# Giving SyncE's transfers the program-order edge that the other engines' instructions have, in a one-core hybrid decoder step

## The chip, the cores and the metric

The kernel runs on one core of a Trainium2 chip. The core has a matrix engine (PE, with its weight loads shown apart as PEld), VectorE (DVE), ScalarE (ACT), GpSimd (POOL) and SyncE (SP). In this kernel SP computes nothing: it issues all transfers between the chip's memory and the core's on-chip memory, one after the other, into one hardware queue (SPq in the profile), and 16 DMA engines carry them out. The metric is the device time of one execution in microseconds, the median of three runs; lower is better.

## What is computed

One inference step of a decoder with two layers of width 1024, for a prompt of 1024 rows and a sample group of 8 x 4 rows (1056 rows in all). Both layers are `x <- x + gate * Branch(RMSNorm(x) * (1 + scale) + shift)`; the first branch is attention in a sliding window, the second a gated DeltaNet (gated linear attention in chunks of 64 with a state for each head). Cut to what matters here:

```python
for layer in range(DEPTH):                       # 0: window attention, 1: gated DeltaNet
    hp, gp = modulate(xp, c_prompt, ...); hs, gs = modulate(xs, c_sample, ...)
    if layer % 2 == 0:
        op, kp, vp = swa_branch(hp, w_in, sinks, w_out)                    # prompt
        osm, ks, vs = swa_branch(hs, w_in, sinks, w_out, cache_k, cache_v) # sample, with its cache
    else:
        op, cp, sp = gdn_branch(hp, zeros, zeros, w_in, conv_w, ..., w_out)
        osm, cs, ss = gdn_branch(hs, state_conv, state_s, w_in, conv_w, ..., w_out)
    xp, xs = xp + gp * op, xs + gs * osm
y_prompt, y_sample = rms_norm(xp, final_norm_g), rms_norm(xs, final_norm_g)

# inside a DeltaNet branch, for each of 16 heads and each chunk of 64 rows:
lower = strict_lower((kb @ k.T) * decay)
sol   = triangular_solve(lower + I, [v * beta, kb * exp(g)])
u     = sol_v - sol_k @ S
o     = q_dec @ S + (q @ k.T * decay) @ u
S     = S * exp(g_total) + k_dec.T @ u          # S: 128 x 128 for each head (and each sample row group)
```

The outputs are the two `y`, the new caches, the new convolution states, and the new states `S` of the prompt (16 heads) and of the eight sample sequences (8 x 16 heads, 64 KB each).

## The kernel before

The work runs in stages along the span. From 0 to about 115 us the inputs are loaded and normalised and the first projections run. Up to about 530 us it is layer 0: projections, attention over blocks of 128 rows, the output projection, with its result kept in memory (`x1d`). From about 530 to 1440 us it is the head loop of layer 1: for each of eight pairs of heads the projections of q, k, v and z, the short convolution, the decay tables, the inversion of the 64 x 64 triangles, and the chain over the chunks. From about 1440 us to the end the output projection of layer 1 runs over the nine row blocks twice (heads 0 to 7, stored in `x2d`, then heads 8 to 15, which gives `y`), and beside it the sample states are read, updated and stored.

Every float32 product is made from split operands (a high part cast by ACT, a low part from POOL or DVE, three matmuls), so that a weight tile goes through load `wr`, cast `wh`, difference `wl`.

**What sets the order.** From the attention on, the kernel issues everything through a planner, the class `Core` (line 96). Each instruction passes through `Core.issued` (line 111), which keeps for each engine the time at which it is free and for each tile the times at which it is written and last used, in a model of the engines. Generators (`weave`) yield the time or the condition at which they want to go on (`ready`, `soon`, `idle`), and the planner places their next instruction when the model says that its moment has come. In that model a transfer occupies SP for 0.45 us and is there 2.4 us after its start, SP works in program order, and a transfer that overwrites something that a transfer last used is not made to wait for it (line 124). For PE, ACT, DVE and POOL the order so found is then made binding: lines 145 to 149 add an edge (without a semaphore) from each instruction to the one before it on its engine. For transfers (lines 126 to 128) no such edge is added. Their place in SP's queue is set afterwards by the tile scheduler, which puts an instruction in when its own model finds its operands and its buffer free; two transfers with no tie between them can change places.

On SP a transfer whose operand or buffer isn't ready holds everything behind it in the queue.

**The names that the prediction touches.**

- `wr` (`load_raw`, line 441, and `load_out`, line 2111): raw weight tiles, a ring of four buffers. `wh`, `wl` (`split_w`, line 449) free them.
- `DP` (`decay_blocks`, line 1786): decay tables, 128 x 2 x 2 x 128 for each of four chunk groups, loaded from `gcr` by eight transfers and then worked on by DVE.
- `Ld` (`solve`), `X`, `Xdd`, `Xc` (`invert`, line 1884): the triangles of a head pair are stored to `Ld`, read back as `X` with one triangle on each partition, inverted by DVE, stored to `Xdd`, read back as `Xc`.
- `zl` (`gating`, line 1993): the gate of a chunk group, loaded from `zd`, multiplied in, and stored to `gTd`; one buffer. `of` (`prepare`, line 2198) reads `gTd` back for the output projection, two buffers.
- `xt` (`rows_of`, line 2231; `finish`, line 2245): the rows of a block, loaded from `x1d` or `x2d`, two buffers; stored to `x2d` or to the output `y`.
- `S` in `new_states` (line 2624): sample states, a ring of three buffers (4 heads each, later 8). After a unit is stored, the next `fetch` reads into the buffer that this store empties:

```python
for _ in range(2):
    fetch()
while units:
    fetch()                                     # loads st <- state_gdn_s
    b, h0, n, st = units.pop(0)
    ...                                         # matmul, then DVE S <- S, gtb, ps_mi
    nc.sync.dma_start(S1[b][:, h0:h0 + n], st)  # out_new_s_s <- S
```

and the rows of a block are asked for when the block before the last has been stored:

```python
yield lambda: stored[0] >= b - 1
xt = xts_[b] = x3.tile([P, D], F32, tag="xt", name="xt", bufs=2)
nc.sync.dma_start(xt[0:cs.stop - cs.start], (x2d if part else x1d)[cs])
```

Of the kernel before, what the change touches and what calls it, by code (L numbers as in the profile page):

```python
# [95 lines left out]
class Core:  # L96
# [14 lines left out]
    def issued(self, eng, op, ins, args, kwargs):  # L111
        aps = [a for a in (*args, *kwargs.values()) if hasattr(a, "tensor")]
        outs = [a for a in (kwargs.get("out", aps[0]), kwargs.get("accum_out")) if a is not None]
        srcs = [a for a in aps if not any(a is o for o in outs)]
        n = 1
        for d in outs[0].shape[1:]:
            n *= d
        start = self.free[eng]
        for a in srcs:
            start = max(start, self.after(self.written, a, eng))  # L120
            if a.space == PSUM:
                start = max(start, self.after(self.used, a, eng))
        for a in outs:
            if self.used.get(self.key(a), (0.0, ""))[1] != "sync" or eng != "sync":
                start = max(start, self.after(self.used, a, eng))
        if "dma" in op:
            self.free[eng] = start + 0.45
            end = start + 2.4
        else:
            rate, fixed = {"tensor": (2400 if op == "matmul" and srcs[0].dtype == F32R  # L130
                                      else 1200 if op == "transpose" else 600, 0.004),
                           "scalar": (1200, 0.06 if op == "copy" and srcs[0].space == PSUM else 0.14
                                      if srcs and srcs[0].space == PSUM else 0.18),
                           "vector": (960, 0.13 if op == "scalar_tensor_tensor" else 0.08),
                           "gpsimd": (420, 0.02 if n >= 256 else 0.14)}[eng]
            if op == "matmul" and outs[0].shape[0] <= 64 and srcs[0].dtype == F32:
                rate = 2400 if n <= 64 and outs[0].shape[0] <= 32 else 600 * P / outs[0].shape[0] if self.group != outs[0].offset // outs[0].ap[0][0] else rate
            if eng == "tensor":
                self.group = outs[0].offset // outs[0].ap[0][0]
            if op == "tensor_scalar_mul" and srcs and srcs[0].space != PSUM and eng == "vector":  # L140
                rate = 1920
            if op == "memset":
                rate = 1e9
            end = self.free[eng] = start + fixed + n / rate
            if eng in self.last:
                self.tc.add_manual_dep(ins, self.last[eng],
                                       mybir.DependencyInfo(mybir.DependencyClass.NoSync, mybir.DependencyReason.DATA),
                                       reason="program order")
            self.last[eng] = ins.name
        for a in srcs:  # L150
            self.used[self.key(a)] = max(self.used.get(self.key(a), (0.0, "")), (end, eng))
        for a in outs:
            self.written[self.key(a)] = self.used[self.key(a)] = (end, eng)
# [2565 lines left out]
```

## Time and profile before

| | |
|---|---|
| time, median of 3 runs | 1733.99 us (1732.49 to 1739.18) |
| profiled execution, its own time | 1732.34 us |
| its span, from the first to the last instruction | 1730.6 us |
| mean granted clock of PE | 0.982 |
| moved by DMA | 191.82 MB |
| transfers read and written in memory | 144.68 MB read, 47.04 MB written |

How to read it: the profile's page gives each engine's busy time as a share of the span, a picture of the span in 40 slices (each digit the busy share in tenths), the chain of work that ended last, and groups of instructions. Views of the trace show the same for a stretch: the instructions in order of time with what ended the idle time before them, the waits of one engine summed by what it waited for, and the busy time of each engine by window. In all of them L89 is the line of the wrapper through which the planner issues, so instructions are told apart by tile names (out<-in). For SP's queue the second column is the time in which the queue was occupied with issuing, for a DMA in the chain of waits it is the time from issue to landing.

### The profile page before, as it was taken

To read this page: it belongs to the slowest core of one execution; us is meant where nothing else is said; L and a number is where in the kernel's file an instruction comes from. 1 tells how busy PE (TensorE), PEld (TensorE's weight loads), DVE (VectorE), ACT (ScalarE), POOL (GpSimd) and SP (SyncE) were. 2 spreads that over 40 slices of the span, in tenths; PEclk is the share of its full clock that TensorE was granted. 3 is DMA by queue.
4 is the path that set the end of the run, shared out by engine and by line. 5 is a ranking of instruction groups with operands and counts; after the bars stand their busy time and mean duration, and the time that the engine had idled before them with its cause. 6 is when DMAs were issued, how large, how long until landed. Compare 5 with 4: busy or idle time off the path is not lost. (4 is left out here: it accounts for less than half of the span.)

```text
span 1730.6 us, 32224 instructions
## 1 busy us (share of the span) xinstructions
PE 1621.2 (94%) x10666; PEld 1429.5 (83%) x10666; DVE 1174.6 (68%) x3538; ACT 862.6 (50%) x2514; POOL 675.5 (39%) x1576
## 2 busy tenths in 40 slices
PE   6999999999999999589999999999999998989897
PEld 5987888977788889469989999899999996657675
DVE  4426675555565787757878778778697776357676
ACT  5625555453335664166554655554655655332332
POOL 2601121122213356235544654546356565323332
PEclk9999999999999999799999999999999999999998
DMA  9542122234233323122412324224132237764885
GB/s 330 153 133 73 51 58 55 51 103 114 92 122 97 105 55 85 29 68 69 127 42 73 102 58 114 65 69 117 46 104 70 56 93 227 218 190 138 244 268 171
DMA packets 281577, 191.82 MB, mean 111 GB/s; under 512 B 98361, under 2 KB 253881, under 8 KB 281378
## 3 DMA queue, kind: packets, MB, share of 16 engines
q1 hardware_dynamic: 281410, 189.75, 38.2%
q8 instruction: 85, 1.39, 0.3%
q14 instruction: 82, 0.67, 0.1%
HBM read 144.68 MB, written 47.04 MB: 111 GB/s over the span
## 5 line engine op out<-in xcount | busy, mean ns | idle before, releaser
L89 POOL TENSOR_TENSOR wl<-wr,wh 128x128 fp32r<-128x128 f32 x488 | 236.7, 515 | 485.5 <-ACT wh L89 449.4
L89 PE MATMUL ps_pj<-h2hi,wh 128*128 128x384 f32 (+1 forms) x1128 | 379.9, 337 | 0.0
L89 PE MATMUL ps_pj<-h2lo,wh 128*128 128x384 f32 (+1 forms) x1128 | 378.1, 335 | 0.0
L89 PE MATMUL ps_pj<-h2hi,wl 128*128 128x384 f32 (+1 forms) x1128 | 376.8, 334 | 0.0
L89 PEld LDWEIGHTS ps_pj<-h2hi,wh 128*128 128x128 f32 x1128 | 213.2, 189 | 3.1 <-ACT wh L89 0.2
L89 PEld LDWEIGHTS ps_pj<-h2hi,wl 128*128 128x128 f32 x1128 | 213.2, 189 | 2.7 <-POOL wl L89 0.2
L89 PEld LDWEIGHTS ps_pj<-h2lo,wh 128*128 128x128 f32 x1128 | 213.0, 189 | 2.2
L89 POOL TENSOR_TENSOR xt<-xt,y 128x512 f32<-128x512 f32 (+1 forms) x48 | 63.6, 1328 | 194.3 <-DVE y L89 170.4
L89 PE MATMUL ps_pj<-hlo,wh 128*128 128x384 f32 (+1 forms) x360 | 119.1, 331 | 0.0
L89 PE MATMUL ps_pj<-hhi,wh 128*128 128x384 f32 (+1 forms) x360 | 118.4, 329 | 0.0
L89 PE MATMUL ps_pj<-hhi,wl 128*128 128x384 f32 (+1 forms) x360 | 118.1, 328 | 0.0
L89 DVE SCALAR_TENSOR_TENSOR vT<-XR,cT,vT 128x384 f32<-128x384 f32 (+1 forms) x144 | 83.9, 591 | 47.4 <-ACT vT L89 45.3
L89 DVE TENSOR_TENSOR tmp<-X 64x31 f32<-64x31 f32 (+15 forms) x248 | 89.0, 359 | 16.9 <-POOL X L89 13.4
L89 DVE TENSOR_TENSOR X<-X,tmp 64x31 f32<-64x31 f32 (+15 forms) x248 | 90.7, 366 | 8.5
L89 ACT CAST wh<-wr 128x512 fp32r<-128x512 f32 x122 | 75.1, 617 | 16.4 <-PE ps_pj L89 11.3
L89 POOL TENSOR_TENSOR Xd<-Xc,cst 32x128 f32<-32x128 f32 x128 | 62.7, 490 | 40.5 <-DVE UZ L89 24.4
L89 PEld LDWEIGHTS ps_pj<-hlo,wh 128*128 128x128 f32 x360 | 67.7, 188 | 10.5 <-issue 10.5
L89 ACT COPY XR<-ps_pj 128x384 f32<-128x384 f32 (+1 forms) x96 | 43.0, 448 | 59.5 <-PE ps_pj L89 59.4
L89 PEld LDWEIGHTS ps_pj<-hhi,wh 128*128 128x128 f32 x360 | 67.7, 188 | 4.0 <-issue 3.1
L89 ACT ACTIVATE prob<-prob,nm 128x256 f32<-128x256 f32 (+1 forms) x128 | 62.2, 489 | 15.5 <-DVE nm L89 15.3
L89 PEld LDWEIGHTS ps_pj<-hhi,wl 128*128 128x128 f32 x360 | 67.7, 188 | 2.2 <-issue 2.1
L89 ACT ACTIVATE qe<-ps_mi,Eg 128x128 f32<-128x128 f32 x112 | 34.9, 363 | 60.4 <-PE ps_mi L89 60.3
(574 smaller groups left out, 4203.9 us busy)
## 6 DMA issues: line engine op xcount, KB each, us to landing
wr<-in_gdn_w_in SPq DMA_DIRECT2D x96, 256.0 KB
S<-in_state_gdn_s SPq DMA_DIRECT2D x40, 256.0 KB
xt<-in_x_prompt SPq DMA_DIRECT2D x16, 512.0 KB
wm<-in_w_mod SPq DMA_DIRECT2D x16, 512.0 KB
wr<-in_swa_w_in SPq DMA_DIRECT2D x64, 128.0 KB
wmod<-in_w_mod SPq DMA_DIRECT2D x32, 256.0 KB
wm<-in_w_mod SPq DMA_DIRECT2D x32, 256.0 KB
DP<-gcr SPq DMA_DIRECT2D x64, 128.0 KB
```

What stands on the lines that cost most here:

```text
L89: inst = fn(*args, **kwargs)
```

## The change

In the branch for transfers, `Core.issued` now adds the same edge that the other engines' instructions have, to the instruction that the program issued last on the same engine, and notes the transfer as the last one. The planner's model, the times in it and the order of the program are as before.

```diff
         if "dma" in op:
             self.free[eng] = start + 0.45
             end = start + 2.4
+            if eng in self.last:
+                self.tc.add_manual_dep(ins, self.last[eng],
+                                       mybir.DependencyInfo(mybir.DependencyClass.NoSync, mybir.DependencyReason.DATA),
+                                       reason="program order")
+            self.last[eng] = ins.name
         else:
```

What moves: on SP the order changes almost everywhere from the attention on. On PE, DVE, ACT and POOL the order from there on is the same; ahead of it (up to about 115 us, outside the planner) a gate step and half of the sample rows' v transposes come some 28 instructions earlier. Three places of SP's queue follow, the operand names as in the list above.

SP, end of the program before (the last rows; `S_...` are single buffers of sample states, the last `of` loads are further up):

```order
L89 DMA xt<-x2d 128x1024
L89 DMA of<-gTd 128x4x128
L89 DMA S_20587<-in_state_gdn_s 128x8x128
L89 DMA out_new_s_s<-S_20394 128x8x128
L89 DMA S_20644<-in_state_gdn_s 128x8x128
L89 DMA out_new_s_s<-S_20496 128x8x128
L89 DMA out_y_p<-xt 128x1024
L89 DMA xt<-x2d 32x1024
L89 DMA out_new_s_s<-S_20587 128x8x128
L89 DMA out_y_p<-xt 128x1024
L89 DMA xt<-x2d 128x1024
```

SP, the same place in the change:

```order
L89 DMA out_new_s_s<-S_20332 128x8x128
L89 DMA S_20587<-in_state_gdn_s 128x8x128
L89 DMA out_new_s_s<-S_20394 128x8x128
L89 DMA S_20644<-in_state_gdn_s 128x8x128
L89 DMA out_new_s_s<-S_20496 128x8x128
L89 DMA out_y_p<-xt 128x1024
L89 DMA xt<-x2d 32x1024
L89 DMA of<-gTd 128x4x128 x2
L89 DMA out_new_s_s<-S_20587 128x8x128
L89 DMA out_y_p<-xt 128x1024
L89 DMA xt<-x2d 128x1024
```

The last two `of` loads, those of the last row block, now stand behind the load of the sample rows (`xt<-x2d 32x1024`), and so behind the `out_y_p` store that empties its buffer. In the rows above this place, too, each store is now followed at once by the load into the buffer that it empties.

SP, the first two head pairs of layer 1, before:

```order
L89 DMA Ld<-UZ 32x4x32 x8
L89 DMA zd<-th 128x384
L89 DMA Ld<-UZ 32x4x32 x8
L89 DMA zd<-th 128x384
L89 DMA zl<-zd 128x2x256
L89 DMA wr<-in_gdn_w_in 128x4x128
L89 DMA X<-Ld 64x1024
L89 DMA zd<-th 128x256
L89 DMA smd<-th 128x32
L89 DMA wr<-in_gdn_w_in 128x4x128 x2
```

SP, the same place in the change:

```order
L89 DMA Ld<-UZ 32x4x32 x8
L89 DMA zd<-th 128x384
L89 DMA Ld<-UZ 32x4x32 x8
L89 DMA X<-Ld 64x1024
L89 DMA zd<-th 128x384
L89 DMA zd<-th 128x256
L89 DMA smd<-th 128x32
L89 DMA DP<-gcr 128x256 x8
L89 DMA wr<-in_gdn_w_in 128x4x128 x2
```

`X<-Ld` comes directly behind the stores it reads, and the eight decay loads of the next head pair, of which most stood further up in pieces of two and three, stand together behind it.

SP, the end of layer 0's attention (`kc`, `vc` the sample caches; `wor` and `wr` weights of the output projection; `selt` a constant), before:

```order
L89 DMA wor<-in_swa_w_out 64x512 x10
L89 DMA kc<-in_cache_swa_k 128x2x256 x2
L89 DMA wr<-in_swa_w_out 64x512 x3
L89 DMA vc<-in_cache_swa_v 128x2x256
L89 DMA wr<-in_swa_w_out 64x512 x2
L89 DMA vc<-in_cache_swa_v 128x2x256
L89 DMA selt<-in_cst 128x256
```

SP, the same place in the change:

```order
L89 DMA wor<-in_swa_w_out 64x512 x10
L89 DMA kc<-in_cache_swa_k 128x2x256
L89 DMA vc<-in_cache_swa_v 128x2x256
L89 DMA kc<-in_cache_swa_k 128x2x256
L89 DMA vc<-in_cache_swa_v 128x2x256
L89 DMA selt<-in_cst 128x256
L89 DMA wr<-in_swa_w_out 64x512 x8
```

Eight halves of weight tiles that were loaded among the caches (three of them further up) now come behind `selt`.

## The prediction

> **What bounds the kernel now.** I read the page first: the busy shares, the slices of the DMA engines, and the chain that ended last.
>
> ```profile
> PE 1621.2 (94%) x10666; PEld 1429.5 (83%) x10666; DVE 1174.6 (68%) x3538; ACT 862.6 (50%) x2514; POOL 675.5 (39%) x1576
> DMA  9542122234233323122412324224132237764885
> PE 27%; DMA 5%; DVE 3%; ACT 2%; POOL 2%; issue 2%; SPq 1%; POOLq 0%; ACTq 0%; DVEq 0%
> ```
>
> PE is the bound: 94% busy, 109 us idle in all (1730.6 less 1621.2). The DMA engines are lightly used through most of the span (tenths 1 to 4) and heavily in the last eight slices, from about 1385 us on (7, 7, 6, 4, 8, 8, 5 behind a 3). An order of transfers can only save or cost where PE or its suppliers wait, so the second view is busy time by window.
>
> ```profile
> 0.00:100.00 100.00, 85.77 (x598) 75.22 (x599) 41.74 (x113) 51.90 (x99) 40.03 (x62) 0.98 0.74 238
> 650.00:750.00 100.00, 76.97 (x596) 67.52 (x595) 74.75 (x209) 31.44 (x101) 41.32 (x113) 0.88 0.24 57
> 750.00:1350.00 600.00, 581.17 (x4079) 551.02 (x4080) 466.50 (x1334) 348.06 (x1093) 308.23 (x869) 1.00 0.30 81
> 1450.00:1550.00 100.00, 91.03 (x485) 63.31 (x485) 44.82 (x131) 36.95 (x100) 33.41 (x67) 0.97 0.76 222
> 1600.00:1650.00 50.00, 44.74 (x198) 35.04 (x196) 34.19 (x97) 17.53 (x38) 17.12 (x14) 0.97 0.85 255
> 1650.00:1700.00 50.00, 48.49 (x224) 39.34 (x223) 35.24 (x126) 15.57 (x40) 15.16 (x12) 1.00 0.84 251
> 1700.00:1731.00 31.00, 17.92 (x79) 12.70 (x77) 21.66 (x71) 7.33 (x17) 5.42 (x4) 0.83 0.47 145
> ```
>
> Columns: window, length, busy of PE, PEld, DVE, ACT, POOL, granted clock, DMA share, GB/s. PE loses 14 us at the start, 23 us near 700, 19 us over the 600 us of the head loop behind it, 9 us at 1450 to 1550, and 20 us after 1600, where the DMA engines are 0.84 busy. The waits of PE over the whole span name what it waited for:
>
> ```profile
> PE ps_lg L89 <- DVE UZ L89: 19.0, 6, 16.9
> PE ps_lg L89 <- DMA S<-in_state_gdn_s: 5.3, 3, 2.3
> PE ps_mi L89 <- DMA kc<-in_cache_swa_k: 3.2, 2, 2.7
> ```
>
> Directly it waits little for transfers (8.5 us); its one long wait, 16.9 us, is for DVE's inversion. So the change acts through other engines, and above all through the time in which SP itself stands. The waits of SP's queue over the whole span, and then, in a second view, from 1600 us on:
>
> ```profile
> SPq L89 <- ACT wh L89: 191.0, 54, 16.2
> SPq L89 <- POOL wl L89: 148.6, 77, 5.9
> ```
>
> ```profile
> SPq L89 <- DMA out_new_s_s<-S: 31.9, 12, 7.0
> SPq L89 <- DMA out_y_p<-xt: 20.1, 6, 5.9
> SPq L89 <- DVE xt L89: 11.9, 7, 4.2
> SPq L89 <- DVE S L89: 7.0, 7, 2.2
> SPq L89 <- POOL xt L89: 2.4, 2, 1.5
> ```
>
> In the last 130 us SP already stands 52.0 us for its own stores to land before it can load into the same buffer, although the scheduler put other transfers between many of these pairs.
>
> **The change part by part.** No instruction is added, removed or resized. Of the engines that compute, the order differs only in the first 115 us; I cost that at 0 (from -1 to +1): PE works 85.77 us of the first 100, and the 14 it lacks are its start. What remains is SP's order, in five places.
>
> *Layer 0's output projection.* Eight weight halves come behind `selt`.
>
> ```profile
> 406.53 0.35 SPq L89 DMA_DIRECT2D selt<-in_cst  x1
> 411.94 2.58 SPq L89 DMA_DIRECT2D wr<-in_swa_w_out  x4
> 408.88 1.13 ACT L89 CAST whi<-wr 128x512 fp32r<-128x512 f32 x2
> 421.70 0.62 ACT L89 CAST whi<-wr 128x512 fp32r<-128x512 f32 x1 [2.50 <-DMA wr<-in_swa_w_out]
> ```
>
> Four halves took 2.58 us to issue, so eight take about 5.2, from 407 on. The first pair is issued by about 408.3 and, at some 2.5 us to landing, is there near 410.8, against its cast at 408.88: 1.9 us late. ACT has gaps that absorb part (the 2.50 us before the later cast, which is late already). Between 0 and +3; I take +1.
>
> *Inversion of the first pairs.* `X<-Ld` loses `zd`, `zl` and `wr` from in front of it.
>
> ```profile
> 605.80 0.50 SPq L89 DMA_DIRECT2D X<-Ld  x1
> 612.09 0.18 DVE L89 TENSOR_TENSOR tmp<-X 64x31 f32<-64x31 f32 x1 [5.59 <-POOL X L89]
> 1022.32 4.62 DMA X<-Ld
> 587.58 1.40 SPq L89 DMA_DIRECT2D DP<-gcr  x3
> DVE DP L89 <- DMA DP<-gcr: 2.5, 1, 2.5
> ```
>
> DVE stood 5.59 us until `X` was usable at 612.09, 6.3 us after the issue; another `X<-Ld` landed in 4.62. Without its two neighbours it goes out about 1 us earlier and may land 1.5 us sooner: -2.5. The eight `DP` loads of the next pair now start behind it, at about 608.6, and need 8 x 0.47 = 3.7 us of issue (1.40 us for three); DVE's first work on them came at about 613, so this gives at most 1 us back. Since this chain feeds the 16.9 us wait, I count it in full: from -4 to +1, taken -2.
>
> *Head pairs 2 to 7.* The same pieces. `DP` in one block before its use instead of strewn can make DVE wait; the only such wait before is the 2.5 us above. PE is 97% busy in 750 to 1350 and none of its waits there is a transfer. At most 1 us for each of six pairs, nothing at best: 0 to +6, taken +1. If PE's cover were gone, the whole 2.5 us would count six times, 15 us.
>
> *Start of the output projection, 1440 to 1600.* The stores `x2d<-xt` are now followed at once by the load `xt<-x1d` that waits for them, with state loads and weights behind.
>
> ```profile
> 1508.33 4.45 DMA x2d<-xt
> ```
>
> Each pair holds SP up to 4.45 us; what is queued behind are state loads, for which PE waited 5.3 us before, and `wr`. If one such wait of up to 2.3 us comes back at three blocks, it is +7; nothing if the other loads are early enough. Taken +3.
>
> *The last 130 us.* From the order, twelve stores of states and seven of rows are directly followed by the load into their buffer.
>
> ```profile
> 1598.57 3.02 DMA out_new_s_s<-S
> 1701.75 6.13 DMA out_y_p<-xt
> 1707.89 2.40 DMA xt<-x2d
> 1712.96 3.22 DMA out_y_p<-xt
> 1716.20 3.73 DMA xt<-x2d
> ```
>
> A state store lands in 3.02 (a small one, before the DMA engines are full) to 7.0 us (the longest wait above), a store of rows in 3.22 to 6.13. SP's standing becomes at the least 12 x 3.02 + 7 x 3.22 = 59 us, at the most 12 x 7.0 + 7 x 6.13 = 127, with middles of 5 and 4.7 us 93, against 52.0 before: 41 us more. Of its waits for producers, 11.9 + 7.0 + 2.4 = 21 us can be eaten. So SP falls some 20 us behind. What is late next is `of`, queued behind these pairs:
>
> ```profile
> 1691.09 1.40 SPq L89 DMA_DIRECT2D of<-gTd  x1
> 1703.48 0.61 ACT L89 CAST ohi<-of 128x512 fp32r<-128x512 f32 x1
> 1706.34 0.62 ACT L89 CAST ohi<-of 128x512 fp32r<-128x512 f32 x1 [0.98 <-PE ps_pj L89]
> 1706.00 0.69 DVE L89 TENSOR_TENSOR olo<-of,ohi 128x512 fp32r<-128x512 f32 x1
> 1720.10 1.59 POOL L89 TENSOR_TENSOR xt<-xt,y 128x512 f32<-128x512 f32 x1 [11.72 <-DMA xt<-x2d]
> ```
>
> This `of` was issued by 1692.5 and cast at 1706.34, so about 11 us of the 20 are covered: 9 remain. The last two `of` give a second reading. Even with nothing else late, they now follow `xt<-x2d` of 1707.89 and land near 1711, so the cast of 1703.48 moves to 1711 and `olo` from 1706.00 to about 1712. On DVE the sample rows' addition and the scaling that leads to the `out_y_p` of 1712.96 are in order behind `olo`: 6 us later. That store empties the buffer for the last `xt<-x2d` (1716.20), for which POOL's last addition waited 11.72 us, and the end moves by 6. Bounds +3 (short landings, half of the 6 covered) to +20; taken +9.
>
> A rule of the Trainium skill speaks for less: "DMA: Bandwidth & Descriptors", section "Latency and other measured facts", gives about 2 us as the fixed cost of a DMA. As an estimate from that page, 19 waits of 2 us are 38 us, below the present 52, and the tail would cost its 6 alone, 1743 in all. The trace differs: no store listed above landed in under 3.02 us.
>
> Sum: +1 - 2 + 1 + 3 + 9 = +12, on the profiled execution's 1732.34 us (span 1730.6 and 1.7 around it): 1744.3. The median of the runs stands 1.65 us above that execution, so 1746.
>
> **The rivals.** (a) *The order doesn't matter.* For it: PE is 94% busy, waits 8.5 us for transfers, and SP's standing costs nothing while buffers are full. Against it: the `of` at the end, whose cast has no cover. If the loads that lead reach far enough, the terms shrink to the inversion's -2 and part of the 6: 1733 to 1740, about 1736. By the Trainium skill, "DMA: Bandwidth & Descriptors", section "Issuing engines are not separate DMA queues", the sequencer's time to start a DMA is usually small beside the DMA; by that rule this rival holds. The trace agrees only for issues without a wait (0.33 to 0.5 us each).
>
> (b) *Faster.* The compute order is fixed to a plan that takes SP to be in order; before, transfers that nobody awaits went ahead of awaited ones. The place is the inversion of the first pairs and the state loads: if `X` comes 4 us sooner, the 5.3 us for `S` and the 3.2 us for `kc` go, that is -12.5, and 1721 by the median. Deciding point: store landings under about 3.2 us, so that the tail costs nothing. Against it: 251 to 255 GB/s at 1600 to 1700, where they took up to 7.0.
>
> (c) *Much slower.* SP stands 340 us for `wh` and `wl` in the head loop and before it; in strict order a blocked `wr` holds `zl`, `X<-Ld` and `DP` behind it. If one wait of 5.9 us reaches DVE and PE at each of six pairs, it is +35 on top: 1780. Against it: the planner places each `wr` where its model sees a free buffer, and these waits may fall between needs. It decides if PE in 750 to 1350 drops below about 560 us a window of 600.
>
> That the change doesn't do what it says is excluded by the new rows of SP's queue.
>
> **How the numbers follow.** Forecast 0.52, own range 1737 to 1765 (terms at their ends rarely fall together; all at once would give 1733 to 1771); (a) 0.20; (b) 0.18; (c) 0.10. A measurement here tells about 0.5% from no change, 8.7 us: 1725.3 to 1742.7. Of the forecast 0.07 lies inside it. Slower 0.45 + 0.10 = 0.55, the same 0.20 + 0.07 = 0.27, faster 0.18. The range from 1727 to 1767 leaves out most of (b) and (c)'s upper part, about 0.2.
>
> **What would show it.** Right: SP's waits for `out_new_s_s` and `out_y_p` after 1600 grow from 52 to 80 to 100 us; the last `ohi<-of` casts wait for `of`; the windows from 1600 hold 8 to 10 us more; the wait for `UZ` shrinks to about 15. Wrong: the stretch behind 1600 as long as before, PE waits for transfers in 750 to 1350, or a tail made shorter by stores that land in 3 us.

## The result, and the profile after

The changed kernel took 1786.85 us (median of 4 runs, 1785.03 to 1788.57) against 1736.59 us for the kernel before in the same comparison: a ratio of 1.0291, 95% interval 1.0264 to 1.0319. It is slower by 50 us; the forecast was 1746, and the time lies outside its range of 1727 to 1767. Of the executions reported here two ran far slower at a lower clock (2272.64 us of the kernel before, 2641.97 of the variant that loads the next state later); the ratios leave them out, and for that variant the median given is that of its other three. The profiled execution took 1788.57 us, its span 1786.8 us, so the difference of the spans, 56.2 us, is a little larger than that of the medians.

From the page of the changed kernel, the busy shares and the slices:

```profile
PE 1636.8 (92%) x10666; PEld 1440.0 (81%) x10666; DVE 1171.4 (66%) x3538; ACT 862.7 (48%) x2514; POOL 677.4 (38%) x1576
DMA  9432221233431412032324223232232266645664
```

Same instructions, same bytes; the DMA engines are now less busy in the last eight slices but the first (6 6 6 4 5 6 6 4 instead of 3 7 7 6 4 8 8 5, in tenths). Something holds transfers back there.

To see where the time went I cut the spans at two instructions that both kernels have: the first cast `ohi<-of` on ACT (the output projection begins) and the first such cast of the second half of the heads. Busy time by window, columns as before; first the kernel before:

```profile
0.00:1449.10 1449.10, 1373.75 (x9481) 1243.72 (x9482) 999.34 (x3016) 770.11 (x2292) 587.20 (x1468) 0.99 0.33 92
1449.10:1601.40 152.30, 137.66 (x698) 99.69 (x697) 84.92 (x232) 52.04 (x131) 51.13 (x81) 0.96 0.65 194
1601.40:1730.60 129.20, 109.76 (x489) 86.12 (x487) 90.32 (x291) 40.44 (x93) 37.19 (x28) 0.95 0.75 228
```

And the changed kernel:

```profile
0.00:1455.90 1455.90, 1377.37 (x9481) 1247.18 (x9482) 995.66 (x3016) 770.28 (x2293) 589.24 (x1470) 0.99 0.32 91
1455.90:1619.10 163.20, 142.47 (x709) 101.65 (x708) 85.30 (x233) 51.95 (x131) 50.65 (x79) 0.96 0.61 181
1619.10:1786.80 167.70, 116.95 (x479) 91.13 (x477) 90.46 (x289) 40.48 (x93) 37.51 (x28) 0.87 0.60 178
```

In these two executions 1450 us of prologue, layer 0 and head loop cost 6.8 us more, the first half of the output projection 10.9, the second half 38.5. In this last stretch PE is idle for 50.8 us instead of 19.4 (length less busy time).

What ACT, PE and SP wait for shows the path. The waits of ACT over the span, then of PE over the span, then of SP's queue from 1600 us, all of the changed kernel:

```profile
ACT ohi L89 <- DMA of<-gTd: 87.8, 16, 10.1
```

```profile
PE ps_mi L89 <- ACT kb L89: 27.0, 6, 12.9
PE ps_lg L89 <- DVE UZ L89: 22.9, 10, 15.6
PE ps_mi L89 <- DVE S L89: 12.8, 5, 5.5
```

```profile
SPq L89 <- DMA out_new_s_s<-S: 61.7, 14, 7.4
SPq L89 <- DVE S L89: 29.0, 9, 13.7
SPq L89 <- DMA out_y_p<-xt: 25.7, 7, 5.0
SPq L89 <- DVE xt L89: 15.9, 5, 5.4
SPq L89 <- DMA x2d<-xt: 8.3, 3, 3.3
```

The last 19 us of the first half are in this view of SP. From 1619.1 us, where the last stretch begins, the state stores are 59.8 us and the rows 25.7 as above, 85.5 together, and the long wait for DVE is gone from the row of `S`:

```profile
SPq L89 <- DVE S L89: 14.9, 7, 6.0
```

The first two rows in the kernel before, over the span:

```profile
ACT ohi L89 <- DMA of<-gTd: 12.7, 3, 5.3
PE ps_mi L89 <- ACT kb L89: 6.8, 4, 3.3
```

Now ACT stands 87.8 us (70.3 of them in the last stretch) in front of a transfer that SP issued late, while SP stands 61.7 + 25.7 = 87.4 us for its own stores (52.0 before). Behind the cast, in order on ACT, stands `kb`, the operand of the next state product, and PE waits for that in turn. The longest of these waits, 12.9 us, has more in front of it: ACT stood 10.10 us for an `of`, and then 0.53 and 3.57 us for two weight tiles `wr`, also loaded behind pairs. One row block of the second half, SP's queue of the changed kernel (start, time occupied with issuing):

```profile
1700.53 0.53 SPq L89 DMA_DIRECT2D of<-gTd  x1
1702.44 0.38 SPq L89 DMA_DIRECT2D out_new_s_s<-S  x1
1706.67 0.37 SPq L89 DMA_DIRECT2D S<-in_state_gdn_s  x1
1707.09 0.57 SPq L89 DMA_DIRECT2D out_y_p<-xt  x1
1712.78 0.33 SPq L89 DMA_DIRECT2D xt<-x2d  x1
1713.20 0.39 SPq L89 DMA_DIRECT2D of<-gTd  x1
1713.64 0.50 SPq L89 DMA_DIRECT2D out_new_s_s<-S  x1
1718.93 0.37 SPq L89 DMA_DIRECT2D S<-in_state_gdn_s  x1
1719.39 0.53 SPq L89 DMA_DIRECT2D of<-gTd  x1
```

and on ACT:

```profile
1698.78 0.62 ACT L89 CAST ohi<-of 128x512 fp32r<-128x512 f32 x1 [7.19 <-DMA of<-gTd]
1705.32 0.62 ACT L89 CAST ohi<-of 128x512 fp32r<-128x512 f32 x1 [1.53 <-DMA of<-gTd]
1717.53 0.62 ACT L89 CAST ohi<-of 128x512 fp32r<-128x512 f32 x1 [8.17 <-DMA of<-gTd]
1718.05 0.50 ACT L89 ACTIVATE kb<-K,cst 96x256 fp32r<-96x256 f32 x1
```

Read them together: `out_new_s_s` goes out at 1702.44 and the load into its buffer 4.23 us later; `out_y_p` at 1707.09, its load 5.69 later; the next pair takes 5.29. From one `of` (1700.53) over the next (1713.20) to the third (1719.39) 18.9 us pass, of which SP stands 3.85 + 5.12 + 4.79 = 13.8 us between the end of a store's issue and the load behind it. On ACT one block, first cast to first cast, takes 1717.53 - 1698.78 = 18.75 us. In the kernel before it was 11.9:

```profile
1654.80 0.62 ACT L89 CAST ohi<-of 128x512 fp32r<-128x512 f32 x1 [0.79 <-PE ps_pj L89]
1666.72 0.62 ACT L89 CAST ohi<-of 128x512 fp32r<-128x512 f32 x1 [1.79 <-DVE rsw L89]
```

There these two casts waited for PE or DVE, not for their transfers.

### The profile page after: what moved, and what is told of

Its sections match the earlier page's. It is cut to its first block, busy times and chain, and to the rows that moved or that the text cites. A ratio compares the mean times of both kernels' runs of the same rounds, so it can differ in the third digit from the quotient of the medians.

```text
span 1786.8 us, 32157 instructions
## 1 busy us (share of the span) xinstructions
PE 1636.8 (92%) x10666; PEld 1440.0 (81%) x10666; DVE 1171.4 (66%) x3538; ACT 862.7 (48%) x2514; POOL 677.4 (38%) x1576
## 5 line engine op out<-in xcount | busy, mean ns | idle before, releaser
L89 ACT CAST ohi<-of 128x512 fp32r<-128x512 f32 x32 | 19.8, 617 | 114.5 <-DMA of<-gTd 87.8
```

The source lines that it names most:

```text
L89: inst = fn(*args, **kwargs)
```

## The experiments

The theory to test (A): the loss comes from pairs in SP's queue, a store and directly behind it the load into the buffer that it empties, in the output projection; strict order elsewhere costs nothing. In the variants of the order the added edge hangs on a flag, `strict`, and where a transfer is taken out, it neither gets the edge nor is one drawn from it. Ratios are to the kernel before in the same comparison. The stretches are cut at the same casts as above.

### Strict order up to the output projection, and from there on

```diff
+    nc.strict = False        # second variant: False from the start, True here
     weave(states_times(), "states")
     weave(core(), "core")
```

> Strict order of SP only up to the start of layer 1's output projection (about 1440 us); from there the transfers have no edge, as before. Theory A (the loss is made in the output projection, where each store is followed at once by the load into its buffer and the loads of `of` stand behind such pairs): 1736 to 1746, at most +9 to the kernel before, and from 1600 us on a profile like that of before. Rival B (strict order in the head loop delays weights and gates, and the output projection only inherits it): 1770 or more.

> The reverse: no edge up to the output projection, strict order from there to the end. Theory A: 1775 to 1787, with ACT's cast of `of` waiting 70 to 90 us in all for its transfer. Rival B: 1736 to 1746.

Measured: 1737.20 us for strict order up to there, ratio 1.0009 (0.9991 to 1.0026), no difference that can be told; 1784.41 for strict order from there on, 1.0277 (1.0258 to 1.0297). Nearly the whole loss is in the output projection, and rival B falls. In the second the casts wait 83.3 us for `of`, inside the 70 to 90. SP's waits from 1600 us, in the second variant:

```profile
SPq L89 <- DMA out_new_s_s<-S: 59.9, 14, 6.8
SPq L89 <- DMA out_y_p<-xt: 27.5, 7, 5.2
```

and in the first, where they are close to those of the kernel before (31.9 and 20.1):

```profile
SPq L89 <- DMA out_new_s_s<-S: 29.7, 12, 6.7
SPq L89 <- DMA out_y_p<-xt: 19.9, 6, 5.5
```

### One family of transfers taken out of the order at a time

```diff
+            nc.strict = False
             nc.sync.dma_start(st, S0[b][:, h0:h0 + n])
+            nc.strict = True
```

and likewise around the store of the states; in other variants around the load of `of`, or around the load of `xt` and the stores of rows.

> Strict order everywhere, except that the loads and stores of the sample states in new_states have no edge. Theory A, with the state pairs as the main part (59.8 of the 85.5 us for which SP stands for store landings after 1615 us): 1745 to 1762. Rival C (the row pairs, a store of y and the load of xt, are what holds `of`): 1775 or more.

> Strict order everywhere, except that the loads of `of` have no edge. Theory A as a matter of SP's total standing (the pairs keep SP busy wherever `of` stands): 1760 to 1780. Rival D (only the place of `of` in the queue matters, a load asked for too late): 1736 to 1750.

> Strict order everywhere, except that the loads of xt from x1d and x2d and the stores of the rows (x2d, y) have no edge. Theory A, both kinds of pairs counting by their standing (row pairs 25.7 + 8.3 of the 93.8 us after 1615): 1765 to 1780. Rival C (the row pairs are the main part): 1755 or less.

> Strict order everywhere except for both kinds of pairs at once: the loads and stores of the sample states in new_states, the loads of xt from x1d and x2d, and the stores of the rows have no edge. `of`, the weights, the gates and everything of the head loop stay in strict order. Theory A (the pairs are the whole loss): 1734 to 1746. Rival H (strict order costs something besides the pairs in the output projection, `of` or weights in their own places): 1752 or more.

> The reverse: only these pairs and the loads of `of` are chained among each other; every other transfer, and all of the head loop, is free as before. Theory A: 1772 to 1788, ACT's cast of `of` waiting 70 us or more. Rival H: 1736 to 1752.

| taken out of strict order | median us | ratio (95%) | projection, first half | second half |
|---|---|---|---|---|
| (kernel before) | 1736 | 1 | 152.3 | 129.2 |
| nothing (the change) | 1786.85 | 1.0291 (1.0264 to 1.0319) | 163.2 | 167.7 |
| sample states | 1756.38 | 1.0120 (1.0085 to 1.0155) | 163.1 | 139.4 |
| rows | 1759.11 | 1.0130 (1.0107 to 1.0153) | 152.0 | 149.0 |
| `of` | 1765.65 | 1.0169 (1.0149 to 1.0189) | 157.6 | 151.4 |
| states and rows | 1739.49 | 1.0021 (1.0005 to 1.0036) | 151.3 | 131.0 |
| all but states, rows and `of` | 1770.83 | 1.0205 (1.0177 to 1.0232) | 149.0 | 165.3 |

The columns of stretches are from the profiled executions: the time between the two casts, and from the second to the end of the span. The profiled execution without the states took 1764.11 us, 8 more than its median.

With both kinds of pairs out and everything else in order, 47 of the 50 us are gone; what is left, 0.2%, is at the limit of what can be told. With the pairs and `of` alone in order, 35 of the 50 us are there (1770.83, just under the 1772 to 1788; the casts wait 80.4 us for `of`), and rival H falls. So the pairs make the loss, together with what stands behind them. In the second half they and `of` suffice (165.3 against 167.7); in the first they do not (149.0 against 163.2).

Each kind by itself is worth more than half: without the states 30.5 us are saved, without the rows 27.7, together 47.4. They serve the same queue, so freeing one may let part of the other's landings pass under its work; that is a reading, not tested. Rival C (rows as the main part) falls with the states' 30.5, but the rows counted for more than I expected: 1759 against 1765 to 1780 (and against 1755 or less for rival C, so neither number was met). Part of the reason stands in the first half, where up to its last 10 us rows are the only part of these pairs: 163.2 us with the rows in order, 152.0 without. What the pair holds up there is open. SP's wait for `x2d` between 1449 and 1615 us is 24.0 us in the changed kernel and 7.2 in the kernel before:

```profile
SPq L89 <- DMA x2d<-xt: 24.0, 6, 5.4
```

But with the pairs and `of` alone in order (last line of the table) SP still stands for `x2d`, from 1449 to 1602 us,

```profile
SPq L89 <- DMA x2d<-xt: 17.4, 6, 4.4
```

the casts wait 13.5 us for `of` there, and the half takes 149.0 us, no longer than before. So neither the landings nor a late `of` are enough to make this part of the loss; the loads that are free in that variant, of weights, gates and old states, have a part in it, and they were not taken apart.

Rival D (only the place of `of` matters) falls with `of` free: its cast then waits 5.1 us instead of 87.8, and 29 us of the loss are still there. SP's waits of that variant from 1600 us, PE's from 1620, and a cast on ACT:

```profile
SPq L89 <- DMA out_new_s_s<-S: 43.1, 12, 5.5
SPq L89 <- DMA out_y_p<-xt: 24.2, 7, 4.4
```

```profile
PE ps_mi L89 <- ACT kb L89: 20.9, 2, 14.3
```

```profile
1629.89 0.62 ACT L89 CAST h2hi<-wr 128x512 fp32r<-128x512 f32 x1 [11.72 <-DMA wr<-in_gdn_w_out]
```

PE still waits for `kb`. For the longest of these waits, 14.3 us, the `kb` of 1635.35 us stands on ACT behind casts of the output projection's weights, and ACT waits 11.72 and 3.83 us for their loads, which stand in SP's queue behind state pairs. With one late supplier mended, the next is late.

### More lead for `of`, in strict order and without

```diff
-                of = x3.tile([P, 4, P], F32, tag="of", name="of", bufs=2)
+                of = x3.tile([P, 4, P], F32, tag="of", name="of", bufs=4)
...
-            for i in (0, 1) if b == 0 else (b + 1,):
+            for i in (0, 1, 2) if b == 0 else (b + 2,):
```

> Strict order everywhere, with four buffers for `of` instead of two, and `of` and xt of a block asked for two blocks ahead instead of one. If lateness of `of` is all that the standing of SP brings (theory A with cover): the casts' wait for `of` falls from 87.8 to under 30 us and the time to 1740 to 1760. Rival G (SP has no more time than its pairs leave, so that more lead only moves the wait to xt or S): 1770 or more.

> The kernel before (no edge) with four buffers for `of` and `of` and xt of a block asked for two blocks ahead. The casts waited 12.7 us for `of` there. If that lead reaches PE: 1726 to 1733, faster than both kernels. If the waits of the others take its place, as in e9: 1733 to 1740, no change.

Measured in strict order: 1780.87 us, ratio 1.0260 (1.0242 to 1.0278). The casts' wait for `of` halved, to 43.3 us (not under 30), but only 6 of the 50 us came back. SP's standing is what it was, 58.1 + 26.6 us against 61.7 + 25.7:

```profile
SPq L89 <- DMA out_new_s_s<-S: 58.1, 14, 6.5
SPq L89 <- DMA out_y_p<-xt: 26.6, 7, 5.2
```

That lies in the range of rival G. In the last stretch the cast now waits for PE instead (`ohi` for `ps_pj` 24.9 us, where it was 9.6); that lead is used up once because the queue has a rate is my reading of it. Without strict order the same lead gives 1737.25, ratio 1.0013 (0.9999 to 1.0027): no gain. No kernel of this study is faster than the one before.

### The load of the next state later

```diff
         while units:
-            fetch()
             b, h0, n, st = units.pop(0)
             for hh in range(n // 2):
+                if hh == n // 4:
+                    fetch()
```

> Strict order everywhere, as in the change, but in new_states the next load is asked for in the middle of the following unit's work instead of directly behind the store, so that other transfers stand between a store and the load into its buffer. Theory A (the standing for store landings is the cost): SP's wait for out_new_s_s falls from 61.7 to under 30 us, time 1745 to 1765. Rival E (strict order couples the queues in any case, the landings are only where it shows): 1775 or more.

Measured: 1775.68 us, ratio 1.0217 (1.0171 to 1.0263). That misses theory A's time and lies at the bound of rival E's. SP's wait for the state stores fell to 45.6 us, not below 30, so about half of the premise was reached; 11 us came back for 16 us less standing. Neither theory is decided by it: whether the landings themselves cost the time, or the strict order in any case, so that the landings are only where it shows, stays open. (The load's new place also moves some instructions of the other engines.)

### A planner that sees the pairs, and another engine for the loads

```diff
-            if self.used.get(self.key(a), (0.0, ""))[1] != "sync" or eng != "sync":
-                start = max(start, self.after(self.used, a, eng))
+            start = max(start, self.after(self.used, a, eng))
```

```diff
-            nc.sync.dma_start(st, S0[b][:, h0:h0 + n])
+            nc.gpsimd.dma_start(st, S0[b][:, h0:h0 + n])
```

> Strict order everywhere, and the planner's exception taken out: a transfer that overwrites what a transfer last used now waits in the model until 2.4 us after that one's start, so the planner sees the pairs as blocking. The order of all engines can move. Theory A': the plan was made blind to the pairs, and a plan that sees part of them puts `of` and the rows ahead: 1745 to 1770. Rival F (the pairs cost the same wherever the plan puts them): 1780 or more.

> Strict order everywhere, but the loads of the sample states in new_states are issued by GpSimd instead of SyncE, so that the wait for a state store's landing holds GpSimd (39% busy) and not the queue with `of`. Theory A: SP's wait for out_new_s_s is gone, 1740 to 1762. Rival I (the wait is as harmful on GpSimd, whose differences and row sums are held instead): 1770 or more.

Measured: 1906.26 us, ratio 1.0972 (1.0941 to 1.1003), and 1840.74, 1.0600 (1.0575 to 1.0625). Both are misses by far, and both say little on the theory, since they move the plan of all engines. With the model's wait in, the head loop itself slows: PE's busy time in 750 to 1350 us, where it was 577.06 in the change:

```profile
750.00:1350.00 600.00, 547.45 (x3698) 504.99 (x3696) 419.73 (x1186) 310.40 (x961) 277.94 (x777) 0.97 0.26 71
```

With the loads on GpSimd SP no longer waits for `out_new_s_s` from 1600 us on, as theory A had it, but the row blocks of the second half come behind most of the states: after the cast `ohi<-of` of 1596.88 us the next is at 1717.67, and from 1609.67 to 1715.74 GpSimd goes from load to load. GpSimd's waits over the span have this row:

```profile
POOL S L89 <- issue: 91.8, 30, 4.2
```

Whether a wait for landing would do less harm on another queue with the plan held fixed was not tried.

## Why the prediction was wrong, point by point

**The direction and the place were right, the size was a quarter of what came.** The last 130 us were to cost 9 us (at most 20) and cost 38.5; the start of the output projection 3 (at most 7) and cost 10.9.

**The standing of SP was right.** From row landings of 3.02 to 7.0 us I had 93 us as the middle for twelve state pairs and seven row pairs, 41 more than before. It came to 87.4, 35.4 more, or 85.5 and 33.5 from the start of the stretch at 1619.1 us.

**The two discounts on it were wrong, and this is the step that failed.** "Of its waits for producers, 11.9 + 7.0 + 2.4 = 21 us can be eaten" took the waits of SP for DVE as slack. They are the same loop seen from the other end. ACT's cast waits for `of` in SP's queue, PE waits for `kb` behind that cast, and DVE stands for the cast's result `ohi`, with its work on `S` and `xt` in order behind; in the last stretch that wait of DVE went from 4.9 to 33.1 us:

```profile
DVE olo L89 <- ACT ohi L89: 33.1, 8, 7.2
```

When SP is late, its producers are later. In the last stretch SP's waits for them did not shrink but grew, from 11.9 to 15.9 us for `xt` and from 7.0 to 14.9 us for `S`. "About 11 us of the 20 are covered" took the lead of `of` over its cast off the sum as if it could be spent on top. The variant with four buffers fits that lead is spent once: twice the lead, 6 us. Without both discounts the sum is 41, or with the measured standing 33.5, against the 38.5 of the stretch; about 7 of those are PE itself (116.95 us busy instead of 109.76, at a granted clock of 0.87 instead of 0.95). That the sizes are near each other does not show that each microsecond of standing costs one: with the later fetch 16 us less of it brought 11, and in the first half of the projection 17.4 us of it, with the other loads free, cost nothing.

**The start of the output projection** had the right place, `x2d` held in front of its load, but priced only state loads and weights behind it, three blocks at 2.3 us. Behind it also stood `of`, for which ACT's cast waited 17.5 us there instead of 3.3; since a wait of 13.5 us cost nothing when the other loads were free, the split of the 10.9 us among `of`, states and weights stays open:

```profile
ACT ohi L89 <- DMA of<-gTd: 17.5, 4, 9.4
```

**The small terms.** `X<-Ld` (issued 609.45) was usable 3.87 us after its issue instead of 6.29, 2.4 us gained where I had 2.5; the `DP` loads behind it gave 1.71 back where I had at most 1; and PE's longest wait for `UZ` went from 16.9 to 15.6. But the stores that `X<-Ld` reads were themselves issued 3.9 us later than before (the second eight at 604.24 instead of 600.33), so `X` was usable 1.2 us later in the span (613.32 instead of 612.09):

```profile
609.45 0.50 SPq L89 DMA_DIRECT2D X<-Ld  x1
613.32 0.18 DVE L89 TENSOR_TENSOR tmp<-X 64x31 f32<-64x31 f32 x1 [2.91 <-POOL X L89]
615.95 0.35 DVE L89 SCALAR_TENSOR_TENSOR DP<-DP,gc,cst 128x128 f32<-128x128 f32 x1 [1.71 <-DMA DP<-gcr]
```

The weights of layer 0's output projection came later, and ACT's cast waited for them; the first store of that stage moved from 428.50 to 430.85 us, and counted from `selt` by 2.9, at the upper end of the 0 to +3.

Head pairs 2 to 7 cost more than the +1 that I took. Over the span DVE now waits eight times for `DP` instead of once for 2.5 us, and PE is busy 4.1 us less in 750 to 1350 us (581.17 before):

```profile
DVE DP L89 <- DMA DP<-gcr: 20.8, 8, 7.6
750.00:1350.00 600.00, 577.06 (x4038) 547.73 (x4037) 460.77 (x1331) 344.09 (x1084) 306.05 (x865) 0.99 0.30 81
```

The other variants with strict order in the head loop and the plan as it was show the same, PE 576.5 to 578.4 us busy, and those without it 580.0 to 581.1. In the time of the variant with strict order only up to the output projection it can't be told from nothing (ratio 1.0009, at most 1.0026, which is 4.5 us); so "costs nothing" in theory A holds to within that.

**The rivals.** (a) and (b) are out. (c) named 1780, near the measured time, but for another reason: PE in 750 to 1350 us was to fall below 560 us, and it fell to 577.06. Its nearness is chance.

**The price from a page.** The Trainium skill, "DMA: Bandwidth & Descriptors", gives about 2 us as the fixed cost of a DMA in "Latency and other measured facts", and by that, as the prediction estimated, the tail would have cost 6. It cost 38.5: a state store held SP for up to 7.4 us here. The same page of the Trainium skill says in "Issuing engines are not separate DMA queues" that the sequencer's time to start a DMA is usually small beside the DMA. That holds here for most issues, of 0.3 to 0.6 us (single ones took up to 2.0), and not for a queue that waits for a landing: with every byte and every transfer unchanged, the order of issue was worth 2.9%.

## What to carry to other kernels

A queue that issues in order is an engine in the loop: where a store is followed directly by the load into its buffer, each pair holds the queue for the landing (13.8 of 18.9 us in the block shown), and everything queued behind is later, however early its data are ready. Whether that costs time depends on what stands behind: it did in the last stretch, and in the first half of the projection not by itself. When two engines wait for each other through buffers, the waits of one are no slack for the other; start the sum from the new standing in full, and take lead off only once for the whole stretch, not for each block. An order from a planner that doesn't count a wait can be paid for on a queue once nothing may reorder it any more: here the free scheduler hid it. Counting that wait in the planner was no cure by itself (1906.26 us).

## What the runs showed of the hardware

A matmul costs more right behind a gap: the state product `ps_mi<-U,kb` takes 0.28 us within a run of matmuls in the kernel before (at 1705.55 us) and 0.55 behind a wait of 3.84 us in the changed one. In the last stretch of the changed kernel the median of these products is 0.28; behind waits of 1.31 and 1.37 us they take 0.39, behind the two longest, of 12.90 and 5.55 us, 0.58 and 0.55.

```profile
1705.55 0.28 PE L89 MATMUL ps_mi<-U,kb 96*128 96x256 f32 x1
```

```profile
1700.78 0.55 PE L89 MATMUL ps_mi<-U,kb 96*128 96x256 f32 x1 [3.84 <-DVE S L89]
```

The Trainium skill, "TensorE: Matmul & The Clock Gate", section "Part 1: The HAM clock gate (the "warmup" mystery)", says that the array falls to half its clock after an idle window of about 3.4 us and needs about as long at work to come back. The mean granted clock of the last stretch, 0.87 against 0.95, with 50.8 us of idle time against 19.4, fits that; the 0.39 us behind waits of under 1.4 us are not explained by it.

The longest wait for a state store's landing was 7.4 us in the changed kernel (a store of 256 KB) and 7.0 before (512 KB). During these two waits the DMA engines carried 188 and 190 GB/s, so they say nothing on what a lighter load would do.
